# A gate pair's front traced in four parts between the running pair's products, and the first output pair's splits ahead of the second standard tile

## The chip, the cores and the metric

The kernel runs on one core of one Trainium2 chip. The metric is the device time of one execution in microseconds (us), as a median over several runs. Five engines work beside each other: PE (TensorE, matrix products and transposes), DVE (VectorE), ACT (ScalarE), POOL (GpSimd) and SP (SyncE, which here only issues transfers).

## What is computed

One layer of a hybrid encoder runs over a prompt of 512 rows and a sample of 1024 rows, both 1024 wide: 12 tiles of 128 rows. Attention and a Fourier mix give, for every row, 1024 columns. What follows concerns the two steps behind them:

```python
h = h + jnp.concatenate([att, fno], axis=-1) @ w_out
gate = jax.nn.sigmoid(rmsnorm(h, ple_norm_g) @ w_ple_gate)
h = h + gate * (p_i @ w_ple_proj)
return rmsnorm(h, final_norm_g)
```

## The kernel before

Every product is made in float32 from two rounded halves: an operand is split into "h" (a rounded copy, `split`, L55, cast by ACT) and "l" (the rest, L59, subtracted by DVE), and three matmuls, h·h, h·l and l·h, stand for one (`mm3`, L65 to L68, or `product`, L520 to L528, 12 matmuls of 128x512 for a 512-deep block).

The output projection takes tiles 0 and 1 as standard tiles (`project`, L569 to L584: 48 matmuls each, with the columns cast into `ch` and the sums added at L583). They are steps of `all_fill` (L586 to L616), a generator whose pieces are poured between the last attention scores. Tiles 2 to 11 are taken in pairs by `project_pair` (L805 to L840): 7 block products of 12 matmuls each, in place of 8, on the four column blocks (`cl`) and on their sums and differences (`s1` to `s4`), against weight blocks `w11`, `w21`, `wt4`, `wt1`, `wt2`, `w22`, `wt3`. Its splits stand at its head: `ah`, `al` are the halves of a block, `ahs`, `als` those of a sum. `keep` (L559) stores each finished row block to `hs` and sums its squares. `load_cl` (L534) fetches column blocks from `cT`, `load_sums` (L545) prepared sums of the weights, `load_x` (L549) the residual. Before pair t=4 the gate's small weights `wp` are loaded from `w_ple_proj` (L854) and split.

The gate phase does the same with six pairs of tiles, t = 0 to 10. A pair has a front (L881 to L905): `rows_in` (L859) loads a row block from `hs` (L861) and the per-layer columns `pr` (L863, then cast to `ph`), `normed` (L868, at L870 on ACT) scales the rows, `turn` (L874, at L877) transposes a row block by 2 x 4 transposes into two `tr` banks, and copies (L888, L893), splits, sums and differences follow. The second four transposes of row b take the bank that the sum `f2` (L892) still reads. Then come the products of `gate_pair` (L944 to L989) with the copies of their banks (L954, L961, L964, L971), the small products `per_layer` (L907, matmuls with `wp`), `finish_half` (L913) and `finish_row` (L923, the scaled row at L933 and its store at L935). Ahead of the first gate pair a loop (L992 to L1014) loads and splits seven weight blocks, `w_ple_gate` for three of them and prepared sums `sg` for four, through four shared tiles `raw` (L1005, L1011, L1012).

In this program the order in which the code is written is not the order on the engines: the build sorts the traced instructions of each engine by a list scheduler, with dependences, modelled durations and the order of tracing as its input. Each engine then takes its instructions strictly in that order. The order of tracing also decides which buffers a tile gets, and so which earlier readers it has to wait for. The lists of both kernels that are quoted below are the sorted ones.

Of the kernel before, what the change touches and what calls it, by code (L numbers as in the profile page):

```python
# [32 lines left out]
def block_kernel(ctx, tc, i, yp, ys):  # L33
# [473 lines left out]

    wo, small = None, None
    wb = {}
    pair_cl, x2 = [], []  # L510

    def open_out():
        nonlocal wo, small
# [72 lines left out]
    def all_fill():  # L586
        yield from blocks(["k2", "q2", "g2", "k3", "q3", "g3"])
        yield from blocks(["f0", "f1", "f2", "f3"], (0, 1))
        last = blocks(["f0", "f1", "f2", "f3"], (2,))
        for n in ("11", "12", "21", "22"):  # L590
            wblock(n, f"x*{int(n[0]) - 1}{int(n[1]) - 1}")
        for k in range(KB):
            raw = px.tile([P, D], F32, tag="raw", name="raw", bufs=2)
            nc.sync.dma_start(out=raw, in_=i["w_out"][0][k * P:(k + 1) * P, :])
            for z in range(2):
                wh, wl = wb[f"{k // 4 + 1}{z + 1}"]
                split(wh[:, k % 4], wl[:, k % 4], raw[:, 512 * z:512 * z + 512],
                      lo_eng=("dve", "pool", "dve")[k % 3])
            next(last)
            yield  # L600
        early = [load_cl(t) for t in range(2)]
        yield from last
        open_out()
        for t in range(2):
            yield from project(t, early[t], load_x(t))
            if t == 0:
                for n in ("t4", "t1"):
                    load_sums(n)
            pair_cl.extend(load_cl(t + 2))
            yield  # L610
        x2.append(load_x(2))
        load_sums("t2")
        load_sums("t3")

    heads = {}
# [164 lines left out]
    with ExitStack() as pcx:  # L780
# [21 lines left out]
        def add(out, x0, x1, eng=None):  # L802
            (eng or nc.vector).tensor_tensor(out=out, in0=x0, in1=x1, op=ALU.add)

        def project_pair(t, cl, x):  # L805
            c11, c12, c21, c22 = cl
            a = {n: halves(n) for n in SUMS}
            a["11"] = a["11"][0], c11
            f11, f12, f21, f22 = (c.bitcast(F32) for c in cl)
            f1, f2 = tmp(), tmp()  # L810
            split(*a["12"], f12)
            split(*a["22"], f22)
            add(f1, f21, f22)
            split(*a["s1"], f1)
            sub(f2, f1, f11)
            split(*a["s2"], f2)
            sub(f2, f12, f2)
            split(*a["s4"], f2)
            sub(f1, f11, f21)
            split(*a["s3"], f1)  # L820
            split_own(*a["11"])
            (xa, xb), L, R = x, slice(0, 512), slice(512, 1024)
# [12 lines left out]
            add(xa[:, R], b1, xa[:, R])  # L835
            product(b0, a["s3"], wb["t3"], False)
            add(xb[:, L], b0, xb[:, L])
            add(xb[:, R], b0, xb[:, R])
            for u in range(2):
                keep(t + u, x[u])  # L840

        def raw4():
            return pool.tile([P, D], F32, tag="hn", name="raw", bufs=4)

        for t in range(2, NT, 2):
            if t == 4:
                wp = [[pool.tile([P, D], F32R, tag=f"wp{k}{n}", name=f"wp{k}{n}") for n in "hl"]
# [4 lines left out]
                for k in range(2):  # L852
                    raw = raw4()
                    nc.sync.dma_start(out=raw, in_=i["w_ple_proj"][0][k * P:(k + 1) * P, :])  # L854
                    split(*wp[k], raw)
            project_pair(t, pair_cl if t == 2 else load_cl(t, True),
                         [x2[0] if t == 2 else load_x(t, row(t)), load_x(t + 1, row(t + 1))])

        def rows_in(t):  # L859
            x = row(t)  # L860
            nc.sync.dma_start(out=x, in_=hs[t])  # L861
            pr = pool.tile([P, 2, P], F32, tag="pr", name="pr", bufs=1)
            nc.sync.dma_start(out=pr, in_=i["p_cols"].rearrange("(k p) t -> p k t", p=P)[:, :, t * P:(t + 1) * P])  # L863
            p2 = [pool.tile([P, 2, P], F32R, tag=f"p{n}", name=f"p{n}", bufs=2) for n in "hl"]
            split(*p2, pr)
            return x, p2

        def normed(t, x):  # L868
            hn = raw4()
# [8 lines left out]
                                    identity=ident)  # L878
            return bank.rearrange("p (a b) -> p a b", b=P)

        def front(t, rows=None):  # L881
            (xa, pa), (xb, pb) = rows or (rows_in(t), rows_in(t + 1))
            ga_, gb = normed(t, xa), normed(t + 1, xb)
            a = {n: halves(n) for n in SUMS}
            f21, f11 = (ph.tile([P, 4, P], F32, tag="hi", name="c", bufs=2) for _ in range(2))
            a["11"] = a["11"][0], ph.tile([P, 4, P], F32R, tag="lo", name="al11", bufs=2)
            f1, f2 = tmp(), tmp()
            nc.scalar.copy(out=f11, in_=turn(ga_, 0, tr()))  # L888
            split(*a["11"], f11)
            ps = turn(ga_, 1, tr())  # L890
            split(*a["12"], ps)
            nc.vector.tensor_tensor(out=f2, in0=ps, in1=f11, op=ALU.add)  # L892
            nc.scalar.copy(out=f21, in_=turn(gb, 0, tr()))  # L893
            ps = turn(gb, 1, tr())
            split(*a["22"], ps)
            add(f1, f21, ps)
            split(*a["s1"], f1)

            sub(f2, f2, f1)
            split(*a["s4"], f2)  # L900
            sub(f1, f1, f11)
            split(*a["s2"], f1)
            sub(f11, f11, f21)
            split(*a["s3"], f11)
            return (xa, xb), (pa, pb), (ga_, gb), a  # L905

        def per_layer(p, z):  # L907
            ps, w = acc(), slice(512 * z, 512 * z + 512)
# [33 lines left out]
                    nc.sync.dma_start(out=dst, in_=g[:, w])  # L942

        def gate_pair(t, x, p, g, a):  # L944
            last = t == NT - 2
            (ga_, gb), L, R = g, slice(0, 512), slice(512, 1024)
            ss = pool.tile([P, 8], F32, tag="ss", name="ss", bufs=2)
# [14 lines left out]
            pp = per_layer(p[0], 1)  # L962
            product(b0, a["s2"], wb["t2"], False)
            nc.scalar.copy(out=ga_[:, R], in_=b0)  # L964
            product(b1, a["s4"], wb["22"], False)
            add(ga_[:, R], ga_[:, R], b1)
            done(0, 1, pp)
            finish_row(t, 0, x, g, ss, 2)
            pp = per_layer(p[1], 1)
            product(b0, a["s3"], wb["t3"], False)  # L970
            nc.scalar.copy(out=gb[:, L], in_=b0)  # L971
# [6 lines left out]
            else:  # L978
# [3 lines left out]
                for n in range(2):  # L982
# [8 lines left out]
        first = [rows_in(t) for t in range(2)]  # L991
        for n, tag in (("11", "x*00"), ("21", "x*10"), ("t4", "t4*"), ("t1", "t1*"), ("t2", "x*01"),  # L992
                       ("22", "x*11"), ("t3", "t3*")):
            if n == "t1":
                nxt = front(0, first)
            w = wblock(n, tag)
            for k in range(0, 4, 2):
                raw = raw4().rearrange("p (a b) -> p a b", a=2)
# [15 lines left out]
                                                   op0=ALU.mult, op1=ALU.subtract)  # L1014

        for t in range(0, NT, 2):
            cur = nxt
            if t + 2 < NT:
                nxt = front(t + 2)
            gate_pair(t, *cur)  # L1020

# [66 lines left out]
```

## Time and profile before

| What | Before |
| --- | --- |
| median of 3 runs | 963.13 us (963.09 to 963.24) |
| the profiled execution | 964.62 us, span 962.8 us, mean granted clock 0.992 |
| PE busy | 915.3 us (95%), 4536 matmuls and transposes |
| DVE, ACT, POOL busy | 637.5 us (66%), 449.6 us (47%), 98.5 us (10%) |
| moved by DMA | 175.63 MB, mean 182 GB/s |
| matmuls at L528 (output pairs and gate pairs) | 33.6% of the chain that ended last, from 640 us on |

The profile is one execution. "Busy" is the time in which an engine worked. PEclk is the share of full clock that was granted to PE; 0.50 of it is 1.2 GHz, 1.00 is 2.4 GHz. A row of the timeline gives the start, the duration, the engine, the line, the operation with its output and inputs, and in brackets how long the engine had stood idle before it and what it waited for. The chain that ended last is followed back from the last instruction to whatever released each step.

### The profile page before, as it was taken

What the parts mean: (1) busy time and instruction counts of PE and PEld (TensorE: products, weight loads), DVE (VectorE), ACT (ScalarE), POOL (GpSimd) and SP (SyncE); (2) the same over time, 40 slices, a digit from 0 to 9 for tenths busy, and PEclk for the clock granted to TensorE, in tenths of its full rate; (3) what the DMA queues carried; (4) which work ended last, traced back from release to release, by engine and by line L of the source; (5) the groups of instructions that cost most, each with busy time, mean ns of one, the idle gap of its engine ahead of it and who ended that gap; (6) DMA issues with size and microseconds to landing.
All of it is one profiled execution on the core that took longest, in us unless ns stands there. A gap on an engine that the chain in (4) does not pass through costs nothing.

```text
span 962.8 us, 13087 instructions
## 1 busy us (share of the span) xinstructions
PE 915.3 (95%) x4536; PEld 747.7 (78%) x4536; DVE 637.5 (66%) x1230; ACT 449.6 (47%) x908; POOL 98.5 (10%) x123
## 2 busy tenths in 40 slices
PE   5999999999999999999999999899899998999995
PEld 4788888888887788888877887777678876777774
DVE  4676443057845698597776978973676777767674
ACT  5543311032324475365554656752343566555542
POOL 3100001010000111000112122421000000000000
PEclk9999999999999999999999999999899999999998
DMA  8669889255547844753577567648875471233211
GB/s 296 226 204 338 290 273 316 85 153 154 164 139 208 228 132 150 202 158 94 180 205 213 166 171 249 195 173 312 290 242 183 143 231 55 93 99 99 93 49 44
DMA packets 123315, 175.63 MB, mean 182 GB/s; under 512 B 9385, under 2 KB 76713, under 8 KB 122225
## 3 DMA queue, kind: packets, MB, share of 16 engines
q1 hardware_dynamic: 121280, 170.72, 55.7%
q0 software_dynamic: 1392, 2.63, 0.9%
q10 hardware_dynamic: 576, 1.44, 0.5%
q8 instruction: 36, 0.59, 0.3%
q14 instruction: 31, 0.25, 0.1%
HBM read 114.96 MB, written 59.80 MB: 182 GB/s over the span
## 4 chain that ended last, share of the span: by engine, by line
PE 72%; DMA 10%; DVE 9%; ACT 4%; issue 2%; SPq 1%; POOL 1%; POOLq 0%; DVEq 0%; ACTq 0%
PE acc L147 23%; PE bank L528 11%; PE sc L657 6%; PE acc L66 6%; PE acc L68 6%; PE acc L67 6%; PE tr L684 3%; DMA x<-hs 2%; DMA raw<-sg 2%; PE tr L67 2%; PE tr L66 2%; PE tr L68 2%; PE tr L414 1%; DMA raw<-w_in 1%; PE tr L284 1%
## 5 line engine op out<-in xcount | busy, mean ns | idle before, releaser
L147 PE MATMUL acc<-xh,wch 128*128 128x512 f32 x384 | 152.2, 396 | 0.0
L147 PE MATMUL acc<-xl,wch 128*128 128x512 f32 x384 | 152.1, 396 | 0.0
L147 PE MATMUL acc<-xh,wcl 128*128 128x512 f32 x384 | 151.7, 395 | 0.0
L663 ACT ACTIVATE pt<-pt,mx 128x1024 f32<-128x1024 f32 (+1 forms) x96 | 96.5, 1007 | 62.4 <-DVE mx L660 61.8
L660 DVE CUSTOM_DVE_ANT_0 pt<-sc,tb 128x1024 f32<-128x1024 f32 (+1 forms) x96 | 97.8, 1041 | 20.3 <-PE sc L657 13.6
L147 PEld LDWEIGHTS acc<-xh,wch 128*128 128x128 f32 x384 | 72.2, 188 | 13.7 <-issue 0.2
L147 PEld LDWEIGHTS acc<-xh,wcl 128*128 128x128 f32 x384 | 72.2, 188 | 13.4
L147 PEld LDWEIGHTS acc<-xl,wch 128*128 128x128 f32 x384 | 72.2, 188 | 13.1 <-issue 0.2
L66 PE MATMUL acc<-wnh,xh 128*128 128x512 f32 x192 | 77.1, 402 | 0.5 <-ACT wnh L55 0.5
L67 PE MATMUL acc<-wnl,xh 128*128 128x512 f32 x192 | 76.8, 400 | 0.0
L68 PE MATMUL acc<-wnh,xl 128*128 128x512 f32 x192 | 76.2, 397 | 0.0
L657 PE MATMUL sc<-kk,qq 128*128 128x512 f32 x160 | 65.7, 411 | 2.4 <-DMA kh_p<-hi 1.6
L657 PE MATMUL sc<-kll,qq 128*128 128x512 f32 x160 | 63.9, 399 | 0.0
L55 ACT CAST wth<-tr 128x512 fp32r<-128x512 f32 x80 | 45.4, 582 | 32.0 <-PE tr L684 31.8
L59 DVE TENSOR_TENSOR wtl<-tr,wth 128x512 fp32r<-128x512 f32 x80 | 53.5, 685 | 6.5 <-ACT wth L55 6.4
L679 DVE SCALAR_TENSOR_TENSOR pt<-pt,rc,pt 128x1024 f32<-128x1024 f32 (+1 forms) x48 | 56.0, 1166 | 1.1
L684 PE MATMUL tr<-ident,pt 128*128 128x128 f32 x320 | 48.4, 276 | 5.8 <-DVE g L729 4.2
L684 PEld LDWEIGHTS tr<-ident,pt 128*128 128x128 f32 x320 | 36.6, 140 | 17.1 <-DVE g L729 6.7
L705 POOL TENSOR_TENSOR g<-ot,g 128x256 f32<-128x256 f32 x24 | 20.3, 847 | 287.6 <-ACT ot L704 282.3
L66 PE MATMUL tr<-wth,v 128*128 128x256 f32 x160 | 45.6, 285 | 0.2 <-DVE wtl L59 0.2
L67 PE MATMUL tr<-wtl,v 128*128 128x256 f32 x160 | 45.5, 284 | 0.3 <-DVE wtl L59 0.2
L68 PE MATMUL tr<-wth,v 128*128 128x256 f32 x160 | 45.1, 282 | 0.0
(297 smaller groups left out, 2056.7 us busy)
## 6 DMA issues: line engine op xcount, KB each, us to landing
raw<-w_in SPq DMA_DIRECT2D x28, 512.0 KB, 5.1
x<-x_sample SPq DMA_DIRECT2D x16, 512.0 KB, 4.7
sot<-o SPq DMA_DIRECT2D x16, 512.0 KB, 4.1
cl<-cT SPq DMA_DIRECT2D x24, 256.0 KB, 3.8
hs<-x SPq DMA_DIRECT2D x12, 512.0 KB, 4.4
x<-hs SPq DMA_DIRECT2D x12, 512.0 KB, 3.8
x<-x_prompt SPq DMA_DIRECT2D x8, 512.0 KB, 5.2
wr<-w_out SPq DMA_DIRECT2D x8, 512.0 KB, 5.8
```

The lines of the kernel that those rows point to most:

```text
L55: a = nc.scalar.copy(out=hi, in_=src)
L59: return a, eng.tensor_tensor(out=lo, in0=src, in1=hi.bitcast(F32), op=ALU.subtract)
L66: nc.tensor.matmul(out=out, lhsT=wh, rhs=xh, start=start, stop=False)
L67: nc.tensor.matmul(out=out, lhsT=wh, rhs=xl, start=False, stop=False)
L68: nc.tensor.matmul(out=out, lhsT=wl, rhs=xh, start=False, stop=stop)
L147: nc.tensor.matmul(out=ps, lhsT=a[:, k], rhs=b[c][k // 4][:, k % 4], start=(n == 0), stop=(n == 23))
L528: nc.tensor.matmul(out=out[:, w], lhsT=a[u][:, k], rhs=b[v][:, k, w], start=(start and k == 0 and n == 0), stop=(k == 3 and n == 2), skip_ ...
L657: nc.tensor.matmul(out=pss[c][:, n:n + 512], lhsT=qq[c], rhs=k[c][:, n:n + 512], start=(m == 0), stop=(m == 1))
L660: nc.vector.tensor_tensor_reduce(out=pt[c][:, :T], in0=ps[:, :T], in1=tb[:, off:off + T], scale=-1.0, scalar=3e38, op0=ALU.add, op1=ALU.mi ...
L663: nc.scalar.activation(out=pt[c][:, :T], in_=pt[c][:, :T], func=AF.Exp, scale=-1.0, bias=mx[:, c:c + 1], accum_out=sm[:, c:c + 1])
L679: nc.vector.scalar_tensor_tensor(out=pt[0][:, :T], in0=pt[1][:, :T], scalar=rc[:, 1:2], in1=pt[0][:, :T], op0=ALU.mult, op1=ALU.add)
L684: nc.tensor.transpose(out=ps[:, j * P:(j + 1) * P], in_=pt[0][:, (b + j) * P:(b + j + 1) * P], identity=ident)
```

## The change

1. `all_fill` loads both standard rows first, runs only `project(0)`, and loads the columns of pair t=2 in two ways: tile 2 as before, tile 3 into one tile `c3` in a slot of the row tiles. `project_pair` is cut into `left` (the splits, sums and differences) and the products. The splits of pair t=2 are traced first, then `project(1)`, then the load of `wt2`, then the pair's products.
2. `rows_in` takes both row blocks of a pair, with one load of 256 per-layer columns in a slot of the `lo` tiles in place of two loads of 128 columns; `columns` splits them, one half for each row.
3. `front` becomes a generator of four parts. `gate_pair` advances it for the next pair: the loads at its own start; row a's `normed` and transposes after the copy of the product with `wt2`; row b's after `finish_row` of row a; the remaining sums and splits at its end. `s2` is split before `s4`.

```diff
     def all_fill():
...
-        for t in range(2):
-            yield from project(t, early[t], load_x(t))
-            if t == 0:
-                for n in ("t4", "t1"):
-                    load_sums(n)
-            pair_cl.extend(load_cl(t + 2))
-            yield
-        x2.append(load_x(2))
-        load_sums("t2")
+        rows = [load_x(t) for t in range(2)]
+        yield from project(0, early[0], rows[0])
+        for n in ("t4", "t1"):
+            load_sums(n)
+        pair_cl.extend(load_cl(2))
+        whole = wo.tile([P, KB, P], F32, tag="x", name="c3", bufs=3)
+        nc.sync.dma_start(out=whole, in_=cT[0].rearrange("(k p) t -> p k t", p=P)[:, :, 3 * P:4 * P])
+        pair_cl.extend([whole[:, 0:4], whole[:, 4:8]])
+        second.append((1, early[1], rows[1]))
         load_sums("t3")
...
+        a = left(pair_cl)
+        run(project(*second[0]))
+        load_sums("t2")
         for t in range(2, NT, 2):
...
-            project_pair(t, pair_cl if t == 2 else load_cl(t, True),
-                         [x2[0] if t == 2 else load_x(t, row(t)), load_x(t + 1, row(t + 1))])
+            if t > 2:
+                a = left(load_cl(t, True))
+            project_pair(t, a, [load_x(t, row(t)), load_x(t + 1, row(t + 1))])
...
         def rows_in(t):
-            x = row(t)
-            nc.sync.dma_start(out=x, in_=hs[t])
-            pr = pool.tile([P, 2, P], F32, tag="pr", name="pr", bufs=1)
-            nc.sync.dma_start(out=pr, in_=i["p_cols"].rearrange("(k p) t -> p k t", p=P)[:, :, t * P:(t + 1) * P])
+            x = [row(t), row(t + 1)]
+            for u in range(2):
+                nc.sync.dma_start(out=x[u], in_=hs[t + u])
+            al11 = ph.tile([P, 4, P], F32R, tag="lo", name="al11", bufs=2)
+            pr = ph.tile([P, 2, 2 * P], F32, tag="lo", name="pr", bufs=2)
+            nc.sync.dma_start(out=pr, in_=i["p_cols"].rearrange("(k p) t -> p k t", p=P)[
+                :, :, t * P:(t + 2) * P])
+            return x, al11, pr
...
-        def front(t, rows=None):
-            (xa, pa), (xb, pb) = rows or (rows_in(t), rows_in(t + 1))
-            ga_, gb = normed(t, xa), normed(t + 1, xb)
+        def front(t):
+            (xa, xb), al11, pr = rows_in(t)
+            yield
+            ga_ = normed(t, xa)
...
             nc.vector.tensor_tensor(out=f2, in0=ps, in1=f11, op=ALU.add)
+            pa = columns(pr, 0)
+            yield
+            gb = normed(t + 1, xb)
             nc.scalar.copy(out=f21, in_=turn(gb, 0, tr()))
             ps = turn(gb, 1, tr())
             split(*a["22"], ps)
             add(f1, f21, ps)
+            yield
             split(*a["s1"], f1)
...
         def gate_pair(t, x, p, g, a):
+            ahead = front(t + 2) if t + 2 < NT else iter(())
+            next(ahead, None)
...
             nc.scalar.copy(out=ga_[:, R], in_=b0)
+            next(ahead, None)
             product(b1, a["s4"], wb["22"], False)
...
             finish_row(t, 0, x, g, ss, 2)
+            next(ahead, None)
             pp = per_layer(p[1], 1)
...
             finish_row(t, 1, x, g, ss, 3 if last else 2)
+            return next(ahead, None)
```

What this does to the sorted order shows at three places. Ahead of them, up to the last attention transposes at about 655 us, the orders are the same.

**PE, end of the scores.** Before, from the norm of the last attention pair (transposes L714) into `project(1)`, which runs on to the pair's products:

```order
L66 MATMUL acc<-w12h,ch 128x512
L67 MATMUL acc<-w12l,ch 128x512
L68 MATMUL acc<-w12h,cl 128x512
L714 MATMUL tr<-ident,ot 128x128 x2
L66 MATMUL acc<-w21h,ch 128x512
L67 MATMUL acc<-w21l,ch 128x512
```

After, from the last value product (`tr`) to the pair's first products (`ah_6619` is the half of `a["12"]`, `ah_6610` that of `a["11"]`):

```order
L68 MATMUL tr<-wth,v_5683 128x256
L714 MATMUL tr<-ident,ot 128x128 x2
L727 MATMUL tr<-ident,ms 128x128 x2
L528 MATMUL bank<-w21h,ah_6619 128x512
L528 MATMUL bank<-w21l,ah_6619 128x512
L528 MATMUL bank<-w21h,al_6620 128x512
L528 MATMUL bank<-w21h,ah_6619 128x512
L528 MATMUL bank<-w11h,ah_6610 128x512
L528 MATMUL bank<-w11l,ah_6610 128x512
L528 MATMUL bank<-w21l,ah_6619 128x512
```

The 12 products of `project(1)` that stood ahead of the value products and the 36 that stood around the two norm transposes now stand behind 20 products of pair t=2.

**ACT, the same place.** Before, the casts of pair t=2 and of `wp`, with the casts `ch` of `project(1)` long done:

```order
L55 CAST ah_6691<-cl 128x512
L55 CAST ahs_6687<-tmp 128x512
L55 CAST ahs_6689<-tmp 128x512
L55 CAST ahs_6693<-tmp 128x512
L55 CAST ahs_6697<-tmp 128x512
L55 CAST wp0h<-raw 128x1024
L55 CAST wp1h<-raw 128x1024
```

After, with the casts `ch` that `project(1)` starts with:

```order
L55 CAST ah_6610<-cl 128x512
L856 DMA gfin<-final_norm_g 128x1024
L55 CAST ahs_6617<-tmp 128x512
L55 CAST ahs_6621<-tmp 128x512
L55 CAST wp0h<-raw 128x1024
L55 CAST ch<-cl 128x512 x2
L55 CAST wp1h<-raw 128x1024
```

The two casts `ch` of `project(1)` now stand behind that of `wp0h`, which needs the transfer of `w_ple_proj`.

**SP, loads ahead of the first gate pair.** Before:

```order
L861 DMA x<-hs_134 128x1024
L861 DMA x<-hs_135 128x1024
L1005 DMA raw<-w_ple_gate 128x2x512 x2
L1005 DMA raw<-sg_149 128x1024 x2
L863 DMA pr<-p_cols 128x2x128 x2
```

After:

```order
L870 DMA x<-hs_134 128x1024
L873 DMA pr<-p_cols 128x2x256
L1032 DMA raw<-w_ple_gate 128x2x512
L870 DMA x<-hs_135 128x1024
L1032 DMA raw<-w_ple_gate 128x2x512
L1032 DMA raw<-sg_149 128x1024 x2
```

The first load of `w_ple_gate` of this piece now stands ahead of the row load `x<-hs_135`, and one load of `pr` ahead of it takes the place of two behind it.

**PE and ACT, the gate pair t=4.** PE before, with the last eight transposes of the next pair's front in the middle of the product with `wt2`:

```order
L528 MATMUL bank<-wt2l,ahs_7893 128x512
L528 MATMUL bank<-wt2h,als_7894 128x512
L877 MATMUL tr<-ident,raw 128x128 x8
L528 MATMUL bank<-wt2h,ahs_7893 128x512
L528 MATMUL bank<-wt2l,ahs_7893 128x512
```

PE after, where they stand behind the product with `w22`:

```order
L528 MATMUL bank<-w22l,ahs_7971 128x512
L528 MATMUL bank<-w22h,als_7972 128x512
L891 MATMUL tr<-ident,raw 128x128 x8
L66 MATMUL acc<-wp0h,ph 128x512
L67 MATMUL acc<-wp0l,ph 128x512
```

ACT after, around the scaling of row b (the second L884):

```order
L984 COPY raw<-bank 128x512
L55 CAST ph<-pr 128x256
L884 ACTIVATE raw<-x,small 128x1024
L987 COPY raw<-bank 128x512
L904 COPY c<-tr 128x512
L55 CAST ah_8437<-tr 128x512
L55 CAST ah_8428<-c 128x512
L912 COPY c<-tr 128x512
```

Row a's eight transposes likewise moved, from the product with `wt1` to behind the product with `wt2`, and row b's scaling (L884) now stands ahead of the copies (L904, L912) out of row a's transposes.

## Rows read from the trace of the kernel before

**Rows 1.** The page: busy time of each engine, its share of the span, instructions.

```profile
PE 915.3 (95%) x4536; PEld 747.7 (78%) x4536; DVE 637.5 (66%) x1230; ACT 449.6 (47%) x908; POOL 98.5 (10%) x123
```

**Rows 2.** Waits of PE from 600 to 963 us: total, times, longest.

```profile
PE tr L877 <- ACT raw L870: 7.0, 5, 3.4
PE bank L528 <- ACT ah L55: 4.4, 2, 2.6
...
PE bank L528 <- DVE cl L59: 1.6, 2, 0.8
...
PE acc L66 <- DVE raw L919: 0.8, 2, 0.5
...
PE bank L528 <- DVE al L59: 0.7, 1, 0.7
```

**Rows 3.** Windows of 4 us: busy time per engine, PEclk, DMA share, GB/s.

```profile
680.00:684.00 4.00, 2.76 (x7) 1.81 (x8) 4.00 (x8) 2.21 (x4) 0.00 (x0) 0.66 0.96 384
684.00:688.00 4.00, 4.00 (x11) 3.03 (x11) 1.79 (x3) 1.74 (x3) 0.00 (x0) 0.50 0.39 118
856.00:860.00 4.00, 2.06 (x10) 1.58 (x9) 0.08 (x1) 1.27 (x2) 0.00 (x0) 0.85 0.11 33
860.00:864.00 4.00, 4.00 (x16) 3.29 (x15) 1.98 (x3) 2.15 (x4) 0.00 (x0) 0.72 0.00 0
```

**Rows 4.** Timeline of PE: first products of three blocks of output pair t=4.

```profile
700.06 0.40 PE L528 MATMUL bank<-w11h,ah 128*128 128x512 f32 x1
...
703.95 0.39 PE L528 MATMUL bank<-w21h,ah 128*128 128x512 f32 x1
...
706.75 0.39 PE L528 MATMUL bank<-wt4h,ah 128*128 128x512 f32 x1
```

**Rows 5.** Timeline: the norm of the last attention pair, from `ot` to the store.

```profile
662.10 0.37 ACT L704 COPY ot<-tr 128x256 f32<-128x256 f32 x1 [4.98 <-PE tr L68]
...
664.61 0.38 PE L714 MATMUL tr<-ident,ot 128*128 128x128 f32 x2
...
666.16 0.69 POOL L721 TENSOR_TENSOR ms<-ms,mhalf 128x2 f32<-128x2 f32 x1 [2.88 <-DVE ms L719]
...
670.37 0.38 PE L727 MATMUL tr<-ident,ms 128*128 128x128 f32 x2
...
671.68 0.32 SPq L733 DMA_DIRECT2D cT<-g  x1
```

**Rows 6.** Timeline of SP, DVE and ACT: the loads of `w_ple_proj`, two subtractions, the cast.

```profile
675.65 0.91 SPq L854 DMA_DIRECT2D raw<-w_ple_proj  x2
...
680.36 1.29 DVE L59 TENSOR_TENSOR als<-tmp,ahs 128x512 fp32r<-128x512 f32 x2
...
683.45 1.05 ACT L55 CAST wp0h<-raw 128x1024 fp32r<-128x1024 f32 x1
```

**Rows 7.** Chain that ended last, in order of time: start, us, what.

```profile
672.53 5.79 DMA cl<-cT
```

**Rows 8.** Timeline of SP and PE ahead of the first gate pair.

```profile
783.66 4.78 SPq L861 DMA_DIRECT2D x<-hs  x2
788.55 0.98 SPq L1005 DMA_DIRECT2D raw<-w_ple_gate  x2
...
806.00 1.09 PE L877 MATMUL tr<-ident,raw 128*128 128x128 f32 x8 [3.38 <-ACT raw L870]
```

**Rows 9.** Timeline of gate pair t=4: its start, row b's load, scaling, transposes, copy.

```profile
840.57 0.40 PE L528 MATMUL bank<-w11h,ah 128*128 128x512 f32 x1
...
852.22 0.41 SPq L861 DMA_DIRECT2D x<-hs  x1
...
857.54 1.15 ACT L870 ACTIVATE raw<-x,small 128x1024 f32<-128x1024 f32 x1 [1.92 <-DMA x<-hs]
858.74 1.96 PE L877 MATMUL tr<-ident,raw 128*128 128x128 f32 x8 [1.94 <-ACT raw L870]
859.88 0.58 ACT L893 COPY c<-tr 128x512 f32<-128x512 f32 x1 [1.19 <-PE tr L877]
```

More of the change, by code (lines that the diff above doesn't have):

```diff
@@ L509, in block_kernel @@
     wb = {}
-    pair_cl, x2 = [], []
+    pair_cl, second = [], []
     def open_out():
@@ L803, in add, with left @@
             (eng or nc.vector).tensor_tensor(out=out, in0=x0, in1=x1, op=ALU.add)
-        def project_pair(t, cl, x):
+        def left(cl):
             c11, c12, c21, c22 = cl
@@ L821, in project_pair @@
             split_own(*a["11"])
+            return a
+        def project_pair(t, a, x):
             (xa, xb), L, R = x, slice(0, 512), slice(512, 1024)
@@ L855, in block_kernel, with columns @@
                     split(*wp[k], raw)
-            project_pair(t, pair_cl if t == 2 else load_cl(t, True),
-                         [x2[0] if t == 2 else load_x(t, row(t)), load_x(t + 1, row(t + 1))])
+            if t > 2:
+                a = left(load_cl(t, True))
+            project_pair(t, a, [load_x(t, row(t)), load_x(t + 1, row(t + 1))])
         def rows_in(t):
-            x = row(t)
-            nc.sync.dma_start(out=x, in_=hs[t])
-            pr = pool.tile([P, 2, P], F32, tag="pr", name="pr", bufs=1)
-            nc.sync.dma_start(out=pr, in_=i["p_cols"].rearrange("(k p) t -> p k t", p=P)[:, :, t * P:(t + 1) * P])
+            x = [row(t), row(t + 1)]
[6 more added lines that the diff above has]
+            return x, al11, pr
+        def columns(pr, u):
             p2 = [pool.tile([P, 2, P], F32R, tag=f"p{n}", name=f"p{n}", bufs=2) for n in "hl"]
-            split(*p2, pr)
-            return x, p2
+            split(*p2, pr[:, :, u * P:(u + 1) * P])
+            return p2
         def normed(t, x):
@@ L879, in turn @@
             return bank.rearrange("p (a b) -> p a b", b=P)
-        def front(t, rows=None):
-            (xa, pa), (xb, pb) = rows or (rows_in(t), rows_in(t + 1))
-            ga_, gb = normed(t, xa), normed(t + 1, xb)
+        def front(t):
+            (xa, xb), al11, pr = rows_in(t)
+            yield
+            ga_ = normed(t, xa)
             a = {n: halves(n) for n in SUMS}
+            a["11"] = a["11"][0], al11
             f21, f11 = (ph.tile([P, 4, P], F32, tag="hi", name="c", bufs=2) for _ in range(2))
-            a["11"] = a["11"][0], ph.tile([P, 4, P], F32R, tag="lo", name="al11", bufs=2)
             f1, f2 = tmp(), tmp()
@@ L896, in front @@
             add(f1, f21, ps)
+            yield
             split(*a["s1"], f1)
             sub(f2, f2, f1)
-            split(*a["s4"], f2)
             sub(f1, f1, f11)
             split(*a["s2"], f1)
+            split(*a["s4"], f2)
             sub(f11, f11, f21)
             split(*a["s3"], f11)
-            return (xa, xb), (pa, pb), (ga_, gb), a
+            pb = columns(pr, 1)
+            yield (xa, xb), (pa, pb), (ga_, gb), a
         def per_layer(p, z):
@@ L988, in gate_pair @@
             finish_row(t, 1, x, g, ss, 3 if last else 2)
-        first = [rows_in(t) for t in range(2)]
+            return next(ahead, None)
+        first = front(0)
+        next(first)
         for n, tag in (("11", "x*00"), ("21", "x*10"), ("t4", "t4*"), ("t1", "t1*"), ("t2", "x*01"),
@@ L994, in block_kernel @@
             if n == "t1":
-                nxt = front(0, first)
+                *_, nxt = first
             w = wblock(n, tag)
@@ L1016, in block_kernel @@
         for t in range(0, NT, 2):
[L1017 to L1020, printed above, removed]
+            nxt = gate_pair(t, *nxt)
 def _split12(a):
```

## The prediction

> **What bounds the kernel now.** I read the page first, for who is busy: PE works 95% of the span [rows 1], so a change that adds no arithmetic can only win back what PE stands idle or runs at the low clock. Up to about 655 us the sorted order is unchanged, so I read only what is behind. The list of PE's waits [rows 2] says where it stands: ahead of output pairs, for splits, and ahead of the transposes of the gate fronts. The windows [rows 3] say where the granted clock falls. The pace of a covered stretch is that of two blocks 12 matmuls apart: 706.75 - 703.95 = 2.80 us, 0.233 each [rows 4]; I take 0.231, since a block's first matmul is a little long. The sum is made against the profiled execution, 964.62 us, which lies 1.5 above the median 963.13 of the runs. A measurement of this kernel can tell about 0.2%, 1.9 us, from no change.
>
> **A. First output pair ahead of tile 1.** Before, PE stops 4.4 + 1.6 + 0.7 = 6.7 us for the splits of output pairs [rows 2]: 5.9 of it in pair t=2, between 670 and 684, the last 0.8 behind the start of pair t=4. Its clock is at 1.2 GHz from about 681 to 688: PEclk is 0.66 and 0.50 in two windows [rows 3], which makes 4 x 0.34/0.5 + 4 = 6.7 us at half speed, 3.4 lost. The change lets the splits start earlier and keeps the 48 matmuls of `project(1)` behind them as cover. But it takes that cover away from the norm of the last attention pair. That chain before: `ot` copied at 662.10, transposes at 664.61, the power done at 666.85, the second transposes only at 670.37 behind 24 matmuls, the store at 671.68 [rows 5]. Now 12 matmuls (2.8) fall away ahead of it and all 24 inside it: the first transposes follow the copy at about 659.7, the power ends 2.24 later, and the store goes out 671.68 - 670.37 = 1.31 behind the second transposes [rows 5], at about 663.3, 8.4 earlier. PE stands about 2.5 us in that chain, then does the pair's first 20 products as their splits come (two in 1.29 on DVE [rows 6]).
>
> What decides is the next in line. `project(1)` needs its casts `ch`, which the order puts behind `wp0h` on ACT; that needs `w_ple_proj`, issued behind the store and two row loads: 663.3 + 0.3 + about 1.4 = 665. From issue to landing I have two rows: a column load in the same crowd took 5.79 [rows 7], and `w_ple_proj` itself at most 683.45 - 675.65 = 7.8 [rows 6]. I take the middle, 6.7: landed at 671.7. With 1.05 for `wp0h` [rows 6] and 0.6 for `ch` (a copy of that size takes 0.58 [rows 9]), PE goes on at 673.4. It then has 48 + 64 = 112 matmuls in hand, 25.9 us, and the pair ends at 699.3; before, the next pair began at 700.06 [rows 4]. That is -0.8; the stop of 0.8 behind it falls away too, since the next pair's splits have `project(1)` as cover; I add back 0.3 for the clock after so long an idle stretch, because most of the slow time lies inside waits. **A = -1.3.** Bounds: landing after 5.8 from an issue at 664 gives -3.6 with no slow time; landing after 7.8 from an issue at 665.5, and a clock as long low as before with half of the loss (1.7) outside the wait, gives +1.6.
>
> The window from 680 to 684 shows 384 GB/s with the DMA engines 96% busy [rows 3]. The Trainium skill, "DMA: Bandwidth & Descriptors", section "Where 436 GB/s comes from", has the memory side bind at about 358 GB/s for a core. That speaks against the change: by that figure the same load would, as an estimate, take 6.7 x 384/358 = 7.2 us, and A would be -0.8. The trace disagrees with it, by its 384, so the sum stays by the rows.
>
> The output pairs behind this (702 to 779) keep their order and only shift: 0.
>
> **C. Weights ahead of the first gate pair.** PE stops 3.38 us at 806.00 for the scaling of a row [rows 8], which ACT does behind the cast of the last weight block. That block comes last in a chain of shared tiles: SP is held at the two row loads from 783.66 to 788.44, and only then issues the loads of `w_ple_gate`, from 788.55 on [rows 8]. Now one load of `w_ple_gate` stands ahead of `x<-hs_135`, so it no longer waits for that row's buffer. The gain is at most half of the 4.78 that the two issues take: 2.4. The chain behind it has three more blocks through four tiles, paced by splits of about 1 us each (1.05 for the cast of such a block [rows 6]), so some of it is lost: I take 0.7 of it. **C = -1.7**, bounds -2.5 and 0. What would be late next is the copy out of the transposes; it is one of ACT's, 0.6. The larger `pr` load stands ahead of the block too, but it is 128 KB more in a stretch where SP waits for buffers, and I cost it at nothing; if it isn't covered, it eats the issue time of about 0.5.
>
> **D. Gate pairs.** Gone: of the five waits for the scaling, 7.0 in all, the one of C is 3.38; the other four make 3.6 [rows 2]. At 856 to 864 the clock falls (0.85, 0.72 [rows 3]), about 0.6 + 1.1 = 1.7 lost, behind the 1.94 stop [rows 9]. Two waits for an accumulator, 0.8 in all [rows 2], stay; with transposes closer to them I put them at 1.0.
> New: row b's transposes come behind the product with `w22`. From the pair's start to there PE has 72 block products, 12 small ones and the first eight transposes: 84 x 0.231 + 0.9 = 20.3 us, and 0.45 more to the second four, 20.8. These need row a's bank, free when `f2` has read it. Before, in pair 4, row b's load was issued 852.22 - 840.57 = 11.65 after the start and its scaling ended at 858.69, that is +18.1 [rows 9]. If that stays, row a's copy (0.58 [rows 9]) comes behind that and a bank's copy, then two casts of as much, two subtractions and `f2` of 0.65 each [rows 6], overlapping: an estimate of +21.2 to +21.5. So a wait of 0.4 to 0.7 by that; since `f2` may go ahead of the subtractions I take 0.3 for pairs 2, 4, 6 and 8, and 1.4 for pair 0, whose rows arrive while the weights still load. New waits 4 x 0.3 + 1.4 + 1.0 = 3.6 against 3.6 + 1.7 + 0.8 = 6.1 gone. **D = -2.5.** Bounds: nothing new, -6.1; or 1.3 per pair at five pairs with 0.8 lost to the clock in each of two, 5 x 1.3 + 1.6 + 1.0 - 6.1 = +3.0. Each pair's one load of `pr` in place of two, and the sums moved to the end, lie beside products: 0.
>
> Sum: -1.3 - 1.7 - 2.5 = -5.5, so 959.1 for such a profiled execution, 957.6 against the median.
>
> **The rivals.**
> *1. The front no longer waits at all.* Rows a and b are loaded at the pair's start, so the loads may go out earlier than +11.65 and `f2` be done in time; then D is -6.1, the sum -9.1, and the median 954.0. For it: the transposes moved later in the pair by 25 matmuls (row a) and 18 (row b), 5.8 and 4.2 us, more than any of the four waits, of which the longest is 1.94. Against it: a row buffer comes free only when the previous pair has finished with it, and that has not moved.
> *2. The gate waits only change places*, D = 0: 960.1. For it: the number of operations between scaling and transposes on ACT grows from the order shown.
> *3. Slower: row a's chain stuck behind row b's load.* ACT takes its instructions in order, and now row b's scaling stands ahead of row a's copies. If the load of row b is issued at +13, the scaling ends 1.35 later than above and `f2` too: PE stops 0.3 + 1.35 = 1.65 in each of four pairs, and if the clock falls behind two of these as it did behind the 1.94 stop (1.7 each), D is 4 x 1.65 + 3.4 + 1.4 + 1.0 - 6.1 = +6.3, the sum +3.3, the median 966.4. With the clock unharmed it is 963.0. So it decides from +13 on; the row shows +11.65.
> *4. The change doesn't do what it says*: the buffers keep the first loads where they are, and both A and C stay at 0, with D alone: 960.6. For it, in A: the wait for `w_ple_proj` is new, and eats what the splits win.
>
> **How the numbers follow.** My forecast, with the terms near those above (956 to 959.5), has 0.50; rival 1 has 0.17; rival 2 0.14; rival 4 0.10; rival 3 0.09. Rivals 2 and 4 lie at 960.1 and 960.6, so the range takes them in: up to 961.5 with half of A's upper bound. Below, rival 1 has 954.0 and with A's lower bound less; 953.0 leaves out the smaller part of that. Outside are rival 3 and the edges, 0.2 in all. Below 961.2 (faster by over 0.2%) are forecast, rival 1 and most of 2 and 4: 0.85. Between 961.2 and 965.0: the rest of these and the case of rival 3 without clock loss, 0.09. Above: 0.06.
>
> **What would show it.** In the changed kernel's timeline, PE should stop about 2.5 us at the norm, then wait for `ch` behind `wp0h`, and go on at 673 to 674; the next output pair should begin within 1 us of 698.5 to 699.5 without a stop for its splits. The stop ahead of the first gate pair should be about 1.7 instead of 3.38. In pairs 2 to 8 the stops at row a's transposes should be gone, and stops under 0.7 us should stand at the second four of row b's, waiting for `f2`; the clock should stay near 1.00 from 850 on. The prediction is wrong if PE goes on with `project(1)` later than 676, if row b's load is issued later than +13 in the pairs, or if the clock falls in more than one of them.

## The result: slower by half a per cent

| What | Before | After |
| --- | --- | --- |
| median of 20 runs each, on the same chip | 960.64 us (955.91 to 963.49) | 965.63 us (961.78 to 968.84) |
| ratio after to before | | 1.0052, 95% interval 1.0037 to 1.0068 |
| the profiled execution | 964.62 us, span 962.8 us | 962.86 us, span 961.1 us |
| PE busy in it | 915.3 us | 916.7 us |

The change costs 0.52%, about 5 us; forecast were 957.6 against 963.13, a gain of 5.5. The two profiles say the opposite of the medians. Single executions of this kernel spread over 7 to 8 us. The profile of before shown ahead of the prediction is longer than any of its 20 timed runs, and the profile of after is the third fastest of 20. So each kernel was profiled a second time (956.90 for before, 967.38 for after, on two different chips, where the kernel before has medians of 961.23 and 960.75). These aren't typical either: of before, one profile lies 4.0 us above the median and the other 3.7 below. The stages are compared over both pairs here, and over all fourteen profiles at the end of the experiments.

From all profiles I took four stages out of PE's timeline: from the last attention transposes that wait for a norm (at about 655) to the start of output pair t=6; from there to the start of gate pair t=2; on to that of gate pair t=10; and from that to the end. A pair starts with its first product with `w11`. In after's timeline of PE these four rows are:

```profile
655.59 0.66 PE L684 MATMUL tr<-ident,pt 128*128 128x128 f32 x4 [0.52 <-DVE g L729]
...
724.06 0.40 PE L528 MATMUL bank<-w11h,ah 128*128 128x512 f32 x1
...
813.00 0.40 PE L528 MATMUL bank<-w11h,ah 128*128 128x512 f32 x1
...
925.35 0.40 PE L528 MATMUL bank<-w11h,ah 128*128 128x512 f32 x1
```

The differences of such rows give, in us (the fourth stage runs to the end of the span):

| Stage | before, 1st | before, 2nd | after, 1st | after, 2nd |
| --- | --- | --- | --- | --- |
| 1: scores' end, pairs 2 and 4 | 64.90 | 61.64 | 68.47 | 68.14 |
| 2: pairs 6 to 10, weights, gate pair 0 | 92.51 | 92.09 | 88.94 | 91.11 |
| 3: gate pairs 2 to 8 | 113.46 | 109.98 | 112.35 | 114.05 |
| 4: gate pair 10 and the end | 36.25 | 36.26 | 35.75 | 35.76 |

Stage 1 is 3 to 7 us longer, stage 2 is 1 to 4 shorter, and stage 3 longer by 2 to 4 than in the second profile of before. The first profile of before has 3 us more than the second in stages 1 and 3 each; in stage 3 the kernels below with the front as before agree with the second.

**Stage 1 after.** The timeline of ACT shows what `project(1)` waited for, that of PE the wait, that of SP the issue of the transfer:

```profile
664.93 0.96 SPq L860 DMA_DIRECT2D raw<-w_ple_proj  x2
```

```profile
667.84 1.22 ACT L55 CAST ahs<-tmp 128x512 fp32r<-128x512 f32 x2 [1.87 <-DVE tmp L800]
674.36 1.04 ACT L55 CAST wp0h<-raw 128x1024 fp32r<-128x1024 f32 x1 [5.30 <-DMA raw<-w_ple_proj]
675.31 1.13 ACT L55 CAST ch<-cl 128x512 fp32r<-128x512 f32 x2
```

```profile
660.11 0.44 PE L714 MATMUL tr<-ident,ot 128*128 128x128 f32 x2 [0.52 <-ACT ot L704]
...
662.47 0.43 PE L727 MATMUL tr<-ident,ms 128*128 128x128 f32 x2 [1.91 <-POOL ms L721]
...
665.46 0.80 PE L528 MATMUL bank<-w21h,al 128*128 128x512 f32 x1 [2.09 <-DVE al L59]
...
675.98 0.80 PE L66 MATMUL acc<-w11h,ch 128*128 128x512 f32 x1 [4.57 <-ACT ch L55]
```

ACT has nothing to do for 5.30 us. The casts `ch` have their columns, and a kernel below makes them at 670.15, but here they stand behind a cast whose data lands 9.4 us after its issue. In the windows (columns as in [rows 3]: the busy time of PE, PEld, DVE, ACT and POOL, the granted clock, the DMA share, GB/s) the granted clock falls to 1.2 GHz twice, where [rows 3] had one fall: behind the stop of 2.09 us for `al`, and again behind that of 4.57 for `ch`. The products right behind these stops take 0.80 us in place of 0.39 to 0.40.

```profile
664.00:668.00 4.00, 2.54 (x6) 2.08 (x7) 3.96 (x8) 1.91 (x4) 0.00 (x0) 0.63 0.99 405
668.00:672.00 4.00, 3.41 (x13) 2.20 (x12) 2.21 (x4) 1.06 (x2) 0.00 (x0) 0.95 1.02 407
672.00:676.00 4.00, 0.02 (x1) 0.02 (x1) 0.56 (x1) 1.64 (x3) 0.00 (x0) 0.91 1.05 405
676.00:680.00 4.00, 4.00 (x10) 3.13 (x11) 3.35 (x5) 1.39 (x2) 0.00 (x0) 0.50 0.48 177
680.00:684.00 4.00, 4.00 (x15) 3.17 (x14) 0.34 (x1) 0.62 (x1) 0.00 (x0) 0.74 0.94 304
```

From 676 to 684, where PE is busy throughout, that is 4 x 0.5 + 4 x 0.26 = 3.0 us lost in products.

**Stage 3 after.** PE's waits from 600 us on, to hold against [rows 2]; the first two lines are new:

```profile
PE acc L66 <- ACT ch L55: 4.6, 1, 4.6
PE tr L891 <- DVE tmp L908: 4.0, 4, 1.5
```

The first is the stop in stage 1. Gate pair t=4 shows where the second comes from, in SP's, ACT's, DVE's and PE's timelines (the counterpart of [rows 9]; L908 makes the sum `f2`):

```profile
841.25 0.40 PE L528 MATMUL bank<-w11h,ah 128*128 128x512 f32 x1
...
853.18 1.00 SPq L956 DMA_DIRECT2D y_prompt<-raw  x2
854.28 0.41 SPq L870 DMA_DIRECT2D x<-hs  x1
...
858.07 1.03 PE L891 MATMUL tr<-ident,raw 128*128 128x128 f32 x8
...
858.88 1.15 ACT L884 ACTIVATE raw<-x,small 128x1024 f32<-128x1024 f32 x1 [3.23 <-DMA x<-hs]
859.94 0.57 ACT L987 COPY raw<-bank 128x512 f32<-128x512 f32 x1
860.40 0.59 ACT L904 COPY c<-tr 128x512 f32<-128x512 f32 x1
...
861.51 0.69 DVE L59 TENSOR_TENSOR al<-tr,ah 128x512 fp32r<-128x512 f32 x1 [5.40 <-ACT ah L55]
862.12 0.68 DVE L59 TENSOR_TENSOR al<-c,ah 128x512 fp32r<-128x512 f32 x1
862.72 0.68 DVE L908 TENSOR_TENSOR tmp<-tr,c 128x512 f32<-128x512 f32 x1
863.55 0.63 PE L891 MATMUL tr<-ident,raw 128*128 128x128 f32 x4 [1.20 <-DVE tmp L908]
```

Row a's transposes are done at about 859, but ACT waits 3.23 us for row b's load, scales row b and copies a bank before it copies row a's transposes out at 860.40; then DVE puts two subtractions ahead of `f2`. Row b's load goes out 13.03 us after the pair's start; before it was 11.65 in both profiles (852.22 in [rows 9], 847.62 - 835.97 in the second). SP issues it right behind the store of the previous pair's last row block (853.18), so it is as late as that row block.

**Before, profiled again.** Its waits from 600 us on, its stop ahead of the first gate pair, and its windows behind the norm and around the stretch that had the low clock:

```profile
PE bank L528 <- ACT ah L55: 2.6, 2, 1.8
PE tr L877 <- ACT raw L870: 2.6, 5, 1.1
```

```profile
801.74 1.09 PE L877 MATMUL tr<-ident,raw 128*128 128x128 f32 x8 [1.09 <-ACT raw L870]
```

```profile
672.00:676.00 4.00, 3.95 (x9) 2.99 (x10) 0.69 (x1) 0.49 (x1) 0.48 (x1) 0.57 0.97 307
...
848.00:852.00 4.00, 4.00 (x19) 3.22 (x18) 2.81 (x5) 3.29 (x8) 0.00 (x0) 1.00 0.63 203
852.00:856.00 4.00, 3.72 (x21) 2.88 (x20) 1.51 (x3) 2.49 (x5) 0.00 (x0) 1.00 0.14 37
856.00:860.00 4.00, 4.00 (x19) 3.28 (x18) 3.93 (x7) 1.54 (x3) 0.00 (x0) 1.00 0.00 0
```

The five waits for the scaling make 2.6 us, not 7.0, the longest 1.1, not 3.4, and the clock is full from 848 to 860. It is low for a shorter stretch behind the norm than in [rows 3] (about 1.7 us lost, not 3.4), and a little at 776 to 784 (0.80 and 0.77). The same five waits in the two kernels below that keep the front as before (the first part alone, without and with POOL):

```profile
PE tr L884 <- ACT raw L877: 2.5, 5, 0.8
```

```profile
PE tr L885 <- ACT raw L878: 3.5, 5, 1.7
```

Neither has a low clock between 848 and 872. So much of what terms C and D wanted to win back belonged to the one execution that was read.

### The profile page after: what moved, and what is told of

Its sections match the earlier page's. It is cut to its first block, busy times and chain, and to the rows that moved or that the text cites. A ratio compares the mean times of both kernels' runs of the same rounds, so it can differ in the third digit from the quotient of the medians.

```text
span 961.1 us, 13057 instructions
## 1 busy us (share of the span) xinstructions
PE 916.7 (95%) x4536; PEld 750.2 (78%) x4536; DVE 635.3 (66%) x1230; ACT 450.2 (47%) x908; POOL 101.1 (11%) x123
## 4 chain that ended last, share of the span: by engine, by line
PE 41%; DMA 7%; DVE 5%; ACT 2%; issue 2%; POOL 1%; SPq 1%; POOLq 0%; ACTq 0%; DVEq 0%
PE bank L528 15%; PE acc L147 9%; PE sc L657 4%; DMA x<-hs 3%; PE tr L684 2%; PE acc L66 2%; PE acc L68 2%; PE acc L67 2%; PE tr L66 1%; PE tr L67 1%; PE tr L68 1%; DMA raw<-w_ple_proj 1%; DMA raw<-sg 1%; DMA raw<-w_out 1%; DVE pt L660 1%
## 5 line engine op out<-in xcount | busy, mean ns | idle before, releaser
L147 PEld LDWEIGHTS acc<-xh,wcl 128*128 128x128 f32 x384 | 72.4, 189 | 13.4
```

Source lines behind the costliest of these rows:

```text
L147: nc.tensor.matmul(out=ps, lhsT=a[:, k], rhs=b[c][k // 4][:, k % 4], start=(n == 0), stop=(n == 23))
```

## The experiments

Two theories were held against each other: theory 1, that the loss is in stage 1, by the casts of tile 1 behind `w_ple_proj`; theory 2, that it is in the gate fronts, by the wait for `f2`. Ratios are to the kernel before, measured beside it, with 95% intervals.

**The first part alone.** `all_fill`, `left` and `project_pair` as changed, `rows_in`, `front` and `gate_pair` as before:

```diff
+        a = left(pair_cl)
+        run(project(*second[0]))
+        load_sums("t2")
...
-            project_pair(t, pair_cl if t == 2 else load_cl(t, True),
...
+            if t > 2:
+                a = left(load_cl(t, True))
...
```

> Only the first part of the change: the first output pair's splits ahead of the second standard tile, the fronts as before. Theory 1 (the casts of tile 1 stand behind the cast of w_ple_proj's first half, PE waits some 4.6 us for that and runs slow behind it): slower than the kernel before by 3 to 5 us, ratio 1.003 to 1.005, with the next output pair starting 3 to 5 us later than 700. Theory 2 (the loss lies in the gate pairs, whose transposes now wait for the sum f2): within 1.5 us of the kernel before.

Measured: 1.0034 (1.0016 to 1.0051), 3.3 us slower. The next output pair starts at 703.28, and stage 1 takes 722.65 - 654.91 = 67.74 us. This is as theory 1 expected for this part.

**The front in four parts alone.** `all_fill` and `project_pair` as before:

```diff
+            ahead = front(t + 2) if t + 2 < NT else iter(())
+            next(ahead, None)
```

> Only the front in four parts and the joint loads, the output pairs as before. Theory 1: faster than the kernel before by 1 to 4 us, 3 of it from the stop ahead of the first gate pair. Theory 2: slower by 2 us or more, with stops of 1.1 to 1.5 us for f2 in three or four pairs and the clock low behind some of them.

Measured: 1.0010 (0.9990 to 1.0030). Neither expectation is met: it neither gains nor clearly loses. Stage 2 is 91.62 us, stage 3 112.51, with waits for `f2` of 0.94, 1.84 and 1.17 in three pairs. Against the kernels with the front as before it is shorter in stage 2 and, but for the first profile, longer in stage 3 (table below). The two parts, 3.3 and 1.0 us, add up to 4.3 of the 5.0, though the second can't be told from nothing by itself.

**The split of `w_ple_proj` on POOL**, so that neither ACT nor DVE waits for that transfer ahead of tile 1:

```diff
-                    split(*wp[k], raw)
+                    nc.gpsimd.tensor_copy(out=wp[k][0], in_=raw)
+                    nc.gpsimd.tensor_tensor(out=wp[k][1], in0=raw, in1=wp[k][0].bitcast(F32), op=ALU.subtract)
```

In the changed kernel:

> The changed kernel with both splits of w_ple_proj on POOL, so that neither ACT nor DVE holds tile 1's casts behind that transfer. Theory 1: PE goes on with tile 1 at about 671 in place of 676, and the kernel is 4 to 6 us faster than the changed one, that is 1 us slower to 2 us faster than the kernel before. Theory 2: no more than 1.5 us faster than the changed kernel, since what PE waits for next in that stage is late too.

Measured: 0.9985 (0.9966 to 1.0004), against 1.0052 a gain of 0.67%, 6.4 us, slightly above the 4 to 6 of theory 1. The wait for `ch` is gone, PE goes on with tile 1 at 671.81, stage 1 is 719.10 - 656.20 = 62.90 us. In the first part alone:

> The first part of the change alone (1.0034), with w_ple_proj split on POOL. Theory 1: the casts of tile 1 cost all of that part's loss; PE goes on at about 671, the next output pair starts within 1 us of 699, and the kernel is 4 to 6 us faster than with the first part alone, ratio 0.997 to 0.9995. Rival (the norm's uncovered chain and the clock's fall around it take what the splits win): ratio 1.000 to 1.002.

Measured: 0.9999 (0.9980 to 1.0018), 3.4 us less than without POOL. That lies at the edge between the two expectations: the splits of `w_ple_proj` ahead of tile 1's, on ACT and DVE, are about all of that part's loss, but mended it wins nothing that the interval can tell. The timelines of ACT and POOL of this kernel, with the same transfer landing as late as in after:

```profile
670.15 1.22 ACT L55 CAST ch<-cl 128x512 fp32r<-128x512 f32 x2 [0.59 <-DVE als L59]
```

```profile
674.36 1.04 POOL L861 CAST wp0h<-raw 128x1024 fp32r<-128x1024 f32 x1 [11.43 <-DMA raw<-w_ple_proj]
675.47 2.40 POOL L862 TENSOR_TENSOR wp0l<-raw,wp0h 128x1024 fp32r<-128x1024 f32 x1
```

The casts `ch` run at 670.15 in place of 675.31, and stage 1 takes 62.40 us, inside the 61.64 to 64.90 of the two profiles of before. Much of what it wins on the splits is lost again, since PE stands idle in the norm's chain (0.5 + 1.9 us, as in after) and in the wait for the first `al` (2.1).

**Another slot for tile 1's casts.**

```diff
-    def project(t, cl, x):
-        ch = [wo.tile([P, 4, P], F32R, tag="tmp", name="ch", bufs=2) for _ in range(2)]
+    def project(t, cl, x, ch=None):
+        ch = ch or [wo.tile([P, 4, P], F32R, tag="tmp", name="ch", bufs=2) for _ in range(2)]
...
-        run(project(*second[0]))
+        whole = pool.tile([P, KB, P], F32R, tag="hn", name="ch1", bufs=4)
+        run(project(*second[0], [whole[:, 0:4], whole[:, 4:8]]))
```

> The changed kernel with tile 1's rounded columns in a slot of the raw tiles in place of the two temporaries that the pair's sums use, so that their casts stand ahead of the last two sums and of w_ple_proj. Theory 1: no wait for tile 1's casts above 1 us, no low clock past about 672, 5 to 8 us faster than the changed kernel, so 0 to 4 us faster than the kernel before. Theory 2: as for the POOL kernel, no more than 1.5 us faster than the changed one.

Measured: 1.0009 (0.9994 to 1.0025), 4.1 us faster than the changed kernel, less than expected. The wait for `ch` is gone here too, with `w_ple_proj` still split on ACT and DVE, and stage 1 is 61.83 us. In this profile time goes behind it, in a low clock at 780 to 784 us (0.57) and waits for `f2` of 1.08 to 1.85 us in three pairs.

**Row a's copies on DVE.** The sum `f2` is made first, and the copy and the rounded half that share row a's banks no longer stand behind row b's scaling:

```diff
-            nc.scalar.copy(out=f11, in_=turn(ga_, 0, tr()))
+            nc.vector.tensor_copy(out=f11, in_=turn(ga_, 0, tr()))
...
-            split(*a["12"], ps)
             nc.vector.tensor_tensor(out=f2, in0=ps, in1=f11, op=ALU.add)
+            split(*a["12"], ps, hi_eng="dve")
```

With the front in four parts alone:

> The front in four parts alone (1.001), with row a's copy, half and sum on DVE. Theory 2: 3 to 4.5 us faster than that, ratio 0.9965 to 0.998, with no wait for f2 above 0.4 us and pairs of 27.3 us. Rival: within 1 us of the front alone.

Measured: 0.9976 (0.9960 to 0.9992), 3.3 us less than without. The waits for `f2` are gone, and the pairs from t=4 on take 27.3 us each. Theory 2's mechanism holds for the fronts. The joint loads are still there, so they aren't what costs; the engine of the copies and the earlier place of `f2` were changed together and not tried apart. Row b's load goes out 11.2 to 11.7 us after the start of pairs t=4 to 8 in all five kernels with DVE's copies, and 12.6 to 13.4 in all five profiles with the front in four parts and ACT's. In the changed kernel with POOL:

> The changed kernel with w_ple_proj split on POOL, and in the fronts row a's copy, its second rounded half and the sum f2 made by DVE (f2 first), so that they no longer stand behind row b's scaling on ACT. Theory 2 (each of four pairs is 0.8 to 1 us longer through the wait of row b's second four transposes for f2): those waits fall from 0.8 to 1.9 each to under 0.4, and the kernel is 3 to 4.5 us faster than the one with POOL alone (0.9985), ratio 0.994 to 0.996. Rival (the waits are those for row b's load, and come back at row b's first transposes): within 1 us of the one with POOL alone.

Measured: 0.9973 (0.9957 to 0.9990), only 1.2 us less than with POOL alone: between the two expectations, nearer to the rival's number. The waits for `f2` are gone all the same. But here, and with the front alone too, PE's timeline has a new stop in the first gate pair's front, where DVE is still busy with the last output pair:

```profile
782.59 1.08 PE L892 MATMUL tr<-ident,raw 128*128 128x128 f32 x4 [3.47 <-DVE small L555]
```

**Row a's copies on DVE from the second front on**, so that the first front keeps ACT's:

```diff
-            nc.vector.tensor_copy(out=f11, in_=turn(ga_, 0, tr()))
+            (nc.vector.tensor_copy if t else nc.scalar.copy)(out=f11, in_=turn(ga_, 0, tr()))
...
-            split(*a["12"], ps, hi_eng="dve")
+            split(*a["12"], ps, hi_eng="dve" if t else "act")
```

In the changed kernel with POOL:

> As the kernel with POOL and DVE copies (0.9973), but in the first gate pair's front row a's copy and half stay on ACT, since there DVE is held by the last output pair and PE stood 3.47 us. Theory (that stop and the clock behind it gave back 1.5 to 2 us): 1 to 2.5 us faster, ratio 0.9945 to 0.9965, the stop back to about 1.2 + 0.8 us. Rival (ACT's stops there and the clock cost as much): within 0.7 us of 0.9973.

Measured: 0.9951 (0.9933 to 0.9969). As expected, though the interval reaches into the rival's range. With the slot in place of POOL:

> The same fronts, with tile 1's casts in the raw tiles' slot (1.0009 with the changed kernel's fronts) in place of the POOL splits. By the pair starts the output stage is up to 1 us shorter than with POOL, but the run with it was 2.3 us slower than with POOL; if that was the clock at 780 to 784 and the front's waits, this one comes out within 1 us of the other (0.9945 to 0.9965); if the slot itself costs (raw tiles late), it stays 2 us slower, 0.9965 to 0.998.

Measured: 0.9962 (0.9948 to 0.9976), in the range for a slot that costs nothing; the interval reaches into the other. With the output pairs as before:

> The front in four parts with DVE copies from the second front on, output pairs as before (0.9976 with DVE copies in all fronts). If the first front's stop gave back 1.5 us or more here too: ratio 0.995 to 0.9965, and the first part of the change is worth nothing even when mended; rival: 0.997 to 0.998.

Measured: 0.9945 (0.9931 to 0.9958), median 955.27 against 960.75 beside it: just past the fast end of what was expected, and the lowest ratio of all, without the first part of the change. The intervals of the two kernels ahead of it overlap its own. It beats the kernel before by 5.5 us and, by the ratios, the changed one by 10. Pair t=4's front here, in the timelines of ACT, DVE and PE:

```profile
851.32 1.15 ACT L877 ACTIVATE raw<-x,small 128x1024 f32<-128x1024 f32 x1 [0.53 <-DMA x<-hs]
...
853.21 1.04 PE L884 MATMUL tr<-ident,raw 128*128 128x128 f32 x8
...
853.85 0.69 DVE L897 COPY c<-tr 128x512 f32<-128x512 f32 x1 [2.60 <-PE tr L884]
854.64 0.69 DVE L900 TENSOR_TENSOR tmp<-tr,c 128x512 f32<-128x512 f32 x1
```

DVE copies 0.64 us after row a's transposes began, where ACT took 2.3 us (858.07 to 860.40 in after). Of PE's waits from 600 us on, only one for a scaling is left:

```profile
PE tr L884 <- ACT raw L877: 1.7, 1, 1.7
```

**Both kernels profiled again.** The kernel before:

> The kernel before, profiled once more. If the low clock at 856 to 864 us and the 3.38 us stop ahead of the first gate pair belong to one execution, not to the kernel, they are absent here or stand elsewhere, and its gate pairs are 27.2 to 27.6 us long. If they belong to the kernel, both are there within 1 us of their sizes.

Measured: 956.90 us. The low clock at 856 to 864 is absent, the 3.38 us stop is 1.09: both belonged to one execution. Its gate pairs from t=2 on take 27.1, 27.3, 27.5 and 28.1 us, two of them just outside the expected range. The changed kernel:

> The changed kernel, profiled once more. If its first profile (962.86, third fastest of 20) was a lucky execution, the stop for tile 1's casts is there again at 4 to 5 us with the next output pair at 703 to 705, the waits for f2 stand in three or four pairs with 1.1 to 1.9 us each, and in addition the clock is low somewhere between 780 and 870.

Measured: 967.38 us. The next output pair starts at 705.31, after a stop of 3.06 us for `ch`, shorter than the 4 to 5 expected; the waits for `f2` are 1.26, 1.16, 1.00 and 1.85. The low clock that was expected between 780 and 870 isn't there; its windows are at 1.2 GHz only around 664 to 684, as in the first profile.

Over all fourteen profiles the first stage goes by the output pairs, whatever the front does, and the third by the front, whatever the output pairs do (us):

| Stage 1, by output pairs | Profiles | Mean |
| --- | --- | --- |
| as before | 61.64, 62.47, 63.22, 63.23; 64.90 in the first profile | 63.1 |
| the first part of the change | 68.47, 68.14, 67.74 | 68.1 |
| the same, splits on POOL or own slot | 62.90, 62.40, 62.08, 62.23, 61.83, 62.36 | 62.3 |

| Stage 3 (gate pairs 2 to 8), by front | Profiles | Mean |
| --- | --- | --- |
| as before | 109.98, 110.28, 110.19; 113.46 in the first profile | 111.0 |
| in four parts | 112.35, 114.05, 112.51, 114.39, 114.21 | 113.5 |
| in four parts, copies on DVE | 108.56, 108.61, 108.52, 108.46, 108.48 | 108.5 |

Stage 2 has a mean of 92.5 in the four profiles with the front as before (92.09 to 92.71) and of 90.9 in the five with it in four parts (88.94 to 92.57). By these means the change costs 5.0 in stage 1 and 2.5 in stage 3 and wins 1.6 in stage 2; with the 0.5 of stage 4 that is +5.4, where the medians say +5.0.

## Why the prediction was wrong

The forecast was 957.6 with a range of 953.0 to 961.5 and 0.06 for above 965.0; measured were 965.63. Against the base of 20 runs, 960.64, the change is +5.0 where -5.5 was forecast: 10.5 us amiss, of which the absolute numbers show only 8.0, because the base of three runs was 2.5 too high.

1. **Term A, -1.3, sized wrongly; stage 1 is +5.0 by the means.** The mechanism stood in the prediction: PE idles in the norm's chain (2.5 forecast, 0.52 + 1.91 measured), the store goes out at 663.3 (663.50), `w_ple_proj` is issued at 665 (664.93), and `ch` waits for `wp0h`. What failed is the step from issue to landing: I took 6.7 us, between rows of 5.79 and 7.8, and it was 9.4. The upper bound itself was too short. DMA moved 405 to 407 GB/s with its engines full from 664 to 676; but in before they were as full when this transfer ran (384 GB/s at 680 to 684 [rows 3]), so why it took longer stays open. PE went on at 675.98, not 673.4. The second failed step is "0.3 for the clock": the slow time did not lie inside the wait, 3.0 us of it lay in the products behind it. Together 2.6 + 2.7, which turns -1.3 into +4.0; the first profiles differ by +3.6 in stage 1. Without this wait the term is worth little: the mended order gives 0.9999, whose interval of 1.9 us to either side can't exclude the -1.6 of the sum without its clock, and stage 1 is 0.8 shorter by the means. The base is part of that: the first profile's 6.7 us of stops and its slow clock made stage 1 1.7 to 3.3 us longer than in the four others with the output pairs as before.
2. **Term C, -1.7, about right.** The stop of 3.38 it was to shorten is 1.09 in the second profile of before, and 0.38 and 1.16 in those of after. The load does go out earlier: the first of `w_ple_gate` 3.9 us behind the gate phase's first block product in both profiles of after (789.00 - 785.11), where it was 6.5 and 5.4 in those of before (788.55 - 782.08, 783.96 - 778.59). Stage 2 is 1.0 to 3.6 us shorter in the two pairs and 1.6 by the means; which part of that comes from this load was not tried.
3. **Term D, -2.5, sign wrong; stage 3 is +2.5 by the means.** Its credit side failed: "the other four make 3.6" is 1.5 in the second profile (2.6 less 1.09) and 1.8 in the two kernels with the front as before, and the 1.7 for the clock belonged to one execution, in which row b's scaling began 5.32 us after the issue of its load [rows 9]; in the other it was 3.84 (847.62 to 851.46). Its debit side failed too: "I take 0.3" for the wait for `f2` was 1.1, 1.2, 1.5 and 0.2, in the second profile 1.0 to 1.9. Two steps failed in it: row b's load did not stay at +11.65 but went out at about +13, and `f2` did not go ahead of the subtractions (862.72, behind 861.51 and 862.12). The reason named for the wait, row b's scaling ahead of row a's copies, is right, and moving those copies off ACT, with `f2` ahead of the subtractions, takes 4 to 6 us out of stage 3.
4. **The rivals.** Rival 3 had the mechanism of stage 3: row b's load goes out at +13.03 and +12.86 (857.08 - 844.22), about the point from which it said it decides. Without its clock loss its D is +2.9, near the +2.5. That its number, 966.4, lies so near to the result is luck: its 3.4 us of clock loss in the gate pairs did not come, it kept A at -1.3, and stage 1 made up the rest. Rival 4 named the step that failed in A: the wait for `w_ple_proj` eats what the splits win. No rival had both; rival 3 had 0.09.
5. **The base.** The sum was made against one execution, 964.62, and set off from a median of three runs. Its waits were then treated as the kernel's. The range had nothing for the chance that the waits to be removed are not usually there: those for the scaling are 3.5 to 4.5 us shorter in the three other profiles with the front as before, and the low clock at 856 to 864 is in none of them (they have one between 776 and 792 instead).

## What to carry to other kernels

An engine that takes its instructions in order turns an instruction placed early, but fed by a slow transfer, into a wait for all that stands behind it: look in the sorted order for what stands behind each instruction that needs a transfer, and move that instruction to an engine with nothing behind it. A stop that ends in a transfer, and the low clock after it, should be looked for in a second profile before it is counted as something to win. And a chain that is made late in one loop step can delay the load of the next, as here row b's load stood behind the previous pair's last store, so a wait there comes back.

## What was not expected

- The same kernel's single executions differ by 7 to 8 us in 960 with nothing changed; stops behind transfers and where the granted clock falls differ between two profiles of it (stage 1 by 3.3 us, stage 3 by 3.5).
- By these rows POOL casts a 128x1024 tile in 1.04 us, as fast as ACT's 1.04, but takes 2.40 for the subtraction that DVE does in 1.22 (`wp0l` in the profile of after).
- After an empty stretch of 4.57 us on PE, the clock was at 1.2 GHz for the 4 us window that follows and partly for the next, and the first product then took 0.80 us.
